# Alternating the full and the half products of a wide matrix product, and a pair of one-column products at the head of each MLP quarter

## The chip, the cores and the metric

One core of a Trainium2 chip runs the whole kernel. The metric is the device time of one execution in microseconds. PE is the matrix engine, PEld its weight loading, DVE and ACT the two engines that work on elements, POOL the general one, SP the queue that issues most loads.

## The reference

Two decoder layers over 256 tokens of 2048 features, all in float32. The first layer mixes tokens by gated linear attention, the second by windowed attention with sinks over a shared K/V. Behind each comes an MLP, which holds most of the work:

```python
def rmsnorm(x, g):
    xf = x.astype(jnp.float32)
    y = xf * lax.rsqrt(jnp.mean(xf * xf, axis=-1, keepdims=True) + EPS)
    return (y * g.astype(jnp.float32)).astype(x.dtype)

def sqrelu_mlp(h, w1, w2):
    u = jax.nn.relu(h @ w1)
    return (u * u) @ w2
...
    for layer in range(DEPTH):
        u = rmsnorm(h, norm_mix[layer])
        if layer < N_A:
            h = h + gla_mixer(u, ...)
        else:
            if layer == N_A:
                k_band, v_band = shared_kv(h, ...)
            h = h + swa_sink_mixer(u, k_band, v_band, ...)
        h = h + sqrelu_mlp(rmsnorm(h, norm_mlp[layer]), mlp_w1[layer], mlp_w2[layer])
```

`w1` is 2048 x 8192, `w2` is 8192 x 2048.

## The kernel before

Weights come from memory in blocks of 512 x 512 floats (`ws`, and `wx` and `wy` in the MLP). Each is split in two (`halve`, lines 116 and 117): ACT rounds it to the matrix engine's reduced format (`wh`), DVE takes the difference (`wl`). Activations are split in the same way (`ah`, `al`), and a full-precision product is the sum of three reduced ones, `ah*wh + ah*wl + al*wh`. All products go through the helper `mm` (line 80), so the profile shows them by their tiles: `acc<-act,wh` writes a bank of tag `acc` from activations and the high half. What stands last in such a name need not be the moving operand; the width tells.

The MLP is done in four quarters of its 8192 hidden columns. A quarter has two parts.

*Four wide products* (`gemm_wide`) make 2048 hidden columns, 512 each. A 128 x 128 block of `wh` is the stationary operand, and the two halves of the activations, `ah` and `al`, stand side by side as a moving operand of 512 columns: one full product gives `ah*wh` and `al*wh`. A second one, of 256 columns, adds `ah*wl` to one half of the bank. So each block of weights takes a pair, 512 and 256 columns. A wide product has four column blocks `f`, each with its own bank (`accs[f]`), and 16 row blocks: four steps `kq` of four `k`, hence 64 pairs. Its banks are four of tag `acc`, or two of `tp` and two of `ms` (each of those tags has a ring of two), in turn. At the end `evac_u` (line 830 on) empties each bank: ACT copies (838), DVE adds (839), relu and square follow (843, 844), and splits (847, 848).

*The seven-product part* (`seven`, called twice per quarter) multiplies the hidden columns by `w2`. Half of it is done with seven products of sums of blocks instead of eight: `product(b, o, ws)` adds operand `o` times the block `ws` to bank `b`; DVE forms sums of blocks (line 795, `wy<-wy,ws`). The other half is `plain(i, j, b0, b1)`: hidden block `i` into banks `b0` (first 128 tokens) and `b1`. `A`, `B`, `C` are `acc` banks, `D` a `tp` bank, `E` and `F` the two `ms` banks. All of its products have 512 columns. The last quarter of the second MLP has no such part; there `w2` goes through `gemm_wide` too.

The order of instructions on each engine is set when the program is built: a scheduler goes by its own estimate of when operands and banks come free, with priorities for loads and splits. `later(n, fn)` and `tick()` place small work `n` ticks ahead within the code; a wide product ticks twice in each of its four steps.

Before the change the wide products go in groups of four full products, then the four short ones of the same blocks:

Of the kernel before, what the change touches and what calls it, by code (L numbers as in the profile page):

```python
# [16 lines left out]
P = 128  # L17
# [31 lines left out]
def yoco_kernel(ctx: ExitStack, tc: tile.TileContext, x, norms, mlp_w1, mlp_w2, a_w_in, w_glr, w_gate, a_g_o, a_w_o,  # L49
# [12 lines left out]
    def bank(shape, tag, dtype=F32):  # L62
        return ps[tag].tile(shape, dtype, name=tag, tag=tag)

    def small():
        return bank([P, C], "ms")
# [4 lines left out]
    def later(n, fn):  # L71
        due.setdefault(now[0] + n, []).append(fn)

    def tick():
        now[0] += 1
        for fn in due.pop(now[0], ()):
            fn()

    def mm(o, l, r, start=True, stop=True, **kw):
        nc.tensor.matmul(o, lhsT=l, rhs=r, start=start, stop=stop, **kw)  # L80


    ident = const.tile([P, P], F32, name="ident")
# [3 lines left out]
    ones = const.tile([P, P], F32, name="ones")  # L87
# [34 lines left out]
    def split_w(parts, step=4, queue=nc.sync, between=None):  # L122
        ws = wp.tile([P, 4, C], F32, name="ws", tag="ws", bufs=WS)
        with tc.high_priority(offset=WPRI):
            for k in range(0, 4, step):
                ks = slice(k, k + step)
                o = 0
                for ap in parts:
                    n = ap.shape[1]
                    queue.dma_start(out=ws[:, ks, o:o + n],  # L130
                                    in_=ap[k * P:(k + step) * P].rearrange("(k p) n -> p k n", p=P))
                    o += n
        return halve(ws, o, min(step, 2), between)

    def piece(w, col, n=C):
        return lambda kq: [w[kq * C:(kq + 1) * C, col:col + n]]
# [55 lines left out]
    def gemm_wide(src, act, evac, last=False):  # L192


        accs = []
        tags = wide_tags[0]
        wide_tags.reverse()

        def run(kq):
            if kq == 0:  # L200
                accs.extend(bank([P, 2, T], tag) for tag in tags)
            halves = split_w(src(kq))
            ah, _, a = act[kq]

            groups = [[(k, f) for f in range(4)] for k in range(4)]
            if kq == 0:
                groups = [[(2 * k + i, 2 * h + f) for i in range(2) for f in range(2)] for h in range(2)
                          for k in range(2)]
            if last and kq == 3:
                groups = [[(k, f) for k in range(4)] for f in range(4)]  # L210
            for i, group in enumerate(groups):
                w = [[h[:, f * P:(f + 1) * P] for h in halves[k]] for k, f in group]
                for (k, f), (wh, _) in zip(group, w):
                    mm(accs[f].rearrange("p u t -> p (u t)"), wh, a[:, k].rearrange("p u t -> p (u t)"),
                       kq == 0 and k == 0, False, skip_group_check=True)
                for (k, f), (_, wl) in zip(group, w):
                    mm(accs[f][:, 1], wl, ah[:, k], False, kq == 3 and k == 3, skip_group_check=True)
                if i == 1:
                    tick()
                if last and kq == 3:  # L220
                    evac(i, accs[i])
            tick()
            if kq == 3 and not last:
                for f in range(4):
                    evac(f, accs[f])
        return run

    def go_all(run):
        for kq in range(4):
            run(kq)  # L230


    def new_act():

        a = actp.tile([P, 4, 2, T], F32R, name="act", tag="act")
        return a[:, :, 0], a[:, :, 1], a
# [54 lines left out]
    last = []  # L291
# [379 lines left out]
    def mlp(w1, w2, act, r, gains):  # L671
# [7 lines left out]
        wide_tags.sort()  # L679
        vs = [mp.tile([P, C], F32, name=f"v{n}", bufs=1) for n in range(2)]  # L680

        def new_ops():

            pairs = [actp.tile([P, 2, 2, 4, P], F32R, name="ops", tag="act") for _ in range(2)]
            return [t[:, i] for t in pairs for i in range(2)] + \
                [mp.tile([P, 2, 4, P], F32R, name=f"op{i}", bufs=1) for i in range(3)]

        def combine(op, odd, uf):

            ua, ub = (uf[c] for c in sorted(uf)[-2:]) if odd else (uf[max(uf)], None)  # L690

            def half(i, a):
                nc.scalar.copy(out=op[i][:, 0], in_=a)
                nc.vector.tensor_sub(out=op[i][:, 1], in0=a, in1=op[i].bitcast(F32)[:, 0])

            def less(a, b):
                e = mp.tile([P, 4, P], F32, name="e", tag="e")
                nc.vector.tensor_sub(out=e, in0=a, in1=b)
                return e
            if not odd:  # L700
                half(0, ua[:, :, :P])
                half(6, less(ua[:, :, :P], ua[:, :, P:]))
                return
            e = less(ua[:, :, P:], ub[:, :, P:])
            s = less(ua[:, :, :P], e)
            half(4, e)
            half(2, less(ub[:, :, :P], s))
            half(5, s)
            half(1, ub[:, :, :P])
            half(3, ub[:, :, P:])  # L710
# [110 lines left out]
        for g in range(4):  # L821
            w = w2[g * D:(g + 1) * D]
            seven_of = 0 if g == 3 and not gains else 2
            us, op, uf = {}, None, {}
            for c in range(NC4):
                if c >= seven_of:
                    us[c] = new_act()
                elif c == 0:
                    op = new_ops()
                ms = {}  # L830

                def evac_u(f, acc, c=c, ms=ms):
                    if f % 2 == 0:
                        ms[0] = mp.tile([P, 2, T], F32, name="m", tag="m")
                    if f == 0:
                        uf[c] = mp.tile([P, 4, T], F32, name="u", tag="u")
                    m, j = ms[0], f % 2
                    nc.scalar.copy(out=m[:, j], in_=acc[:, 1])
                    nc.vector.tensor_add(out=m[:, j], in0=acc[:, 0], in1=m[:, j])  # L839
                    if j == 0:  # L840
                        return
                    bs = slice(f - 1, f + 1)
                    nc.vector.scalar_tensor_tensor(out=m, in0=m, scalar=0.0, in1=rb2, op0=ALU.max, op1=ALU.mult)
                    nc.scalar.activation(out=uf[c][:, bs], in_=m, func=AF.Square)
                    if c >= seven_of:
                        ah, al, _ = us[c]
                        nc.scalar.copy(out=ah[:, bs], in_=uf[c][:, bs])
                        nc.vector.tensor_sub(out=al[:, bs], in0=uf[c][:, bs], in1=ah.bitcast(F32)[:, bs])
                    elif f == 3:
                        combine(op, c, uf)  # L850

                go_all(gemm_wide(piece(w1, g * D + c * C), act, evac_u))
            if seven_of:
                for n in range(2):
                    seven(w, n, op, us, g, g == 3 or (g == 2 and not gains), acts, gains if g == 3 else (), sq, nr)
                continue
            for c in range(NC4):
                def evac_x(f, acc, c=c):
                    d = xt[c][:, f]
                    for u in (1, 0):  # L860
                        nc.vector.tensor_add(out=d, in0=acc[:, u], in1=d)
                    r = c * C + f * P
                    nc.sync.dma_start(out=out[r:r + P], in_=d)

                if c % 2 == 0:
                    for i in range(4):
                        later(1 + i, lambda c=c + i // 2, b=i % 2: last_x(c, b, mp))
                go_all(gemm_wide(piece(w, c * C), us, evac_x, c == NC4 - 1))
# [3 lines left out]
    def last_x(c, b, mp):  # L872

        if b == 0:
            xt[c] = mp.tile([P, 4, T], F32, name="xt", tag="u")
        nc.scalar.copy(out=xt[c][:, 2 * b:2 * b + 2], in_=back(c, b))

    (actk, actq), rstd = mlp(mlp_w1[0], mlp_w2[0], actm, rm, (G_KV, G_MIX1))


# [178 lines left out]
    (actm,), rm = residual(b_w_o[0], acta, (G_MLP1,))  # L1059
    sa.close()  # L1060
    mlp(mlp_w1[1], mlp_w2[1], actm, rm, ())


# [41 lines left out]
```

## Time and profile before

| | |
|---|---|
| median of three runs | 2090.39 us (2089.78 to 2093.33) |
| the profiled execution | 2090.28 us, span 2088.6 us |
| PE busy | 2056.3 us, 98% |
| DVE, ACT busy | 1428.7 us, 1146.7 us |
| read from memory | 406.71 MB |

A row of a timeline reads: start in us, length in us, engine, line, operation, what it writes and reads, partitions x elements, count, and in brackets the idle time of the engine ahead of it and what ended that. Several like instructions are merged in a row. Products overlap in the matrix engine, so the length of one is more than its distance to the next. A row of a stretch reads: from and to, its length, PE's busy time (with the number of instructions that touch the stretch), the granted clock of PE, the mean share of the DMA engines, GB/s. A row of waits reads: who waited, for whom, us in total, times, the longest. A row of groups reads: engine, operation, operands, shapes and count, then busy us and mean ns of one, then idle time ahead of it.

### The profile page before, as it was taken

How to read it: one execution, taken by the hardware profiler on the slowest of the kernel's cores; microseconds unless marked ns; L12 is line 12 of the kernel's file. 1: busy time of each engine (PE TensorE's matmuls, PEld its weight loads, DVE VectorE, ACT ScalarE, POOL GpSimd, SP SyncE). 2: the span in 40 equal slices, each digit the busy share in tenths (PEclk: the TensorE clock that was granted, in tenths of full speed). 3: DMA queues.
4: the chain of work that ended last, by engine and by line, in shares of the span. 5: the costliest groups of instructions: out<-in, count | busy, mean ns of one | idle time of the engine just before them, and what ended most of it. 6: DMA issues, size and time to landing. Idle time of an engine off the chain costs nothing.

```text
span 2088.6 us, 26959 instructions
## 1 busy us (share of the span) xinstructions
PE 2056.3 (98%) x10734; PEld 1738.8 (83%) x10734; DVE 1428.7 (68%) x1624; ACT 1146.7 (55%) x1560; POOL 177.0 (8%) x179
## 2 busy tenths in 40 slices
PE   9999999999999999999999999999999999999999
PEld 8988888888888788888877777788788888888888
DVE  6696444567866876786797666656776786787554
ACT  6745445555655555554565676455555555555543
POOL 2262111000000000000001232000000000000000
PEclk9999999999999999999999999999999999999999
DMA  8445555656865785776675443655785686676553
GB/s 278 142 142 180 175 174 176 230 190 189 242 231 189 211 270 184 213 240 213 199 193 157 158 141 112 221 188 185 208 271 184 190 255 222 182 225 198 182 192 130
DMA packets 210654, 410.55 MB, mean 197 GB/s; under 512 B 7024, under 2 KB 15232, under 8 KB 210528
## 3 DMA queue, kind: packets, MB, share of 16 engines
q1 hardware_dynamic: 194704, 377.51, 53.8%
q0 software_dynamic: 15104, 30.23, 8.4%
q8 instruction: 84, 1.38, 0.3%
q10 hardware_dynamic: 720, 1.09, 0.2%
q14 instruction: 42, 0.34, 0.0%
HBM read 406.71 MB, written 2.10 MB: 196 GB/s over the span
## 4 chain that ended last, share of the span: by engine, by line
PE 88%; DVE 7%; ACT 3%; issue 1%; DMA 1%; POOL 0%; SPq 0%; ACTq 0%; POOLq 0%; DVEq 0%
PE acc L80 55%; PE ms L80 19%; PE tp L80 13%; DVE wl L117 3%; ACT sc L998 1%; ACT wh L116 1%; PE tp L610 1%; DVE wy L795 1%; DVE m L839 0%; PE tp L931 0%; DVE st L992 0%; DMA ws<-in_a_w_in_dram 0%; DVE st L994 0%; DMA gk<-in_b_g_q_dram 0%; PE tp L559 0%
## 5 line engine op out<-in xcount | busy, mean ns | idle before, releaser
L117 DVE TENSOR_TENSOR wl<-ws,wh 128x1024 fp32r<-128x1024 f32 (+1 forms) x636 | 780.0, 1234 | 472.5 <-ACT wh L116 467.7
L116 ACT CAST wh<-ws 128x1024 fp32r<-128x1024 f32 (+1 forms) x636 | 659.4, 1040 | 577.0 <-PE acc L80 387.6
L80 PE MATMUL acc<-wh,act 128*128 128x512 f32 x1792 | 575.5, 395 | 0.1
L80 PE MATMUL acc<-act,wh 128*128 128x512 f32 (+1 forms) x1664 | 414.1, 362 | 2.2 <-ACT wh L116 1.4
L80 PEld LDWEIGHTS acc<-wh,act 128*128 128x128 f32 x1792 | 336.2, 188 | 73.0 <-issue 3.6
L80 PE MATMUL acc<-wl,act 128*128 128x512 f32 x896 | 349.8, 391 | 0.0
L80 PEld LDWEIGHTS acc<-act,wh 128*128 128x128 f32 x1664 | 278.9, 190 | 29.7 <-ACT wh L116 1.6
L80 PE MATMUL acc<-act,wl 128*128 128x256 f32 x1408 | 257.6, 282 | 0.6 <-DVE wl L117 0.6
L80 PEld LDWEIGHTS acc<-act,wl 128*128 128x128 f32 x1408 | 227.0, 190 | 26.2 <-DVE wl L117 1.0
L80 PE MATMUL tp<-act,wh 128*128 128x512 f32 x592 | 230.1, 394 | 0.0
L80 PE MATMUL ms<-act,wh 128*128 128x512 f32 x576 | 225.9, 394 | 0.0
L80 PEld LDWEIGHTS acc<-wl,act 128*128 128x128 f32 x896 | 168.8, 188 | 35.3 <-issue 1.7
L117 DVE TENSOR_TENSOR wl<-wx,wh 128x1024 fp32r<-128x1024 f32 x112 | 135.9, 1223 | 73.1 <-ACT wh L116 71.2
L116 ACT CAST wh<-wx 128x1024 fp32r<-128x1024 f32 x112 | 117.7, 1055 | 94.3 <-PE acc L80 52.4
L80 PE MATMUL ms<-act,wl 128*128 128x256 f32 x576 | 148.6, 281 | 0.0
L80 PE MATMUL tp<-act,wl 128*128 128x256 f32 x576 | 148.3, 280 | 0.0
L80 PE MATMUL ms<-wh,act 128*128 128x512 f32 x448 | 146.0, 394 | 0.9
L730 POOL DMA_DIRECT2D wx<-in_mlp_w_dram x28 | 36.1, 1289 | 1128.4 <-DVE wl L117 1026.7
L80 PEld LDWEIGHTS tp<-act,wh 128*128 128x128 f32 x592 | 111.5, 189 | 13.3
L80 PEld LDWEIGHTS ms<-act,wh 128*128 128x128 f32 x576 | 108.6, 189 | 13.6
L80 PEld LDWEIGHTS tp<-act,wl 128*128 128x128 f32 x576 | 108.3, 189 | 12.7
L80 PEld LDWEIGHTS ms<-act,wl 128*128 128x128 f32 x576 | 108.5, 189 | 11.9
(231 smaller groups left out, 2242.9 us busy)
## 6 DMA issues: line engine op xcount, KB each, us to landing
ws<-in_mlp_w_dram SPq DMA_DIRECT2D x228, 1024.0 KB, 5.2
ws<-in_a_w_in_dram SPq DMA_DIRECT2D x44, 1024.0 KB, 5.1
wx<-in_mlp_w_dram POOLq DMA_DIRECT2D x28, 1024.0 KB, 8.9
ws<-in_a_w_o_dram SPq DMA_DIRECT2D x16, 1024.0 KB, 5.0
ws<-in_b_w_q_dram SPq DMA_DIRECT2D x16, 1024.0 KB, 5.0
ws<-in_b_w_o_dram SPq DMA_DIRECT2D x16, 1024.0 KB, 5.0
wx<-in_mlp_w_dram SPq DMA_DIRECT2D x14, 1024.0 KB, 5.1
wy<-in_mlp_w_dram SPq DMA_DIRECT2D x14, 1024.0 KB, 7.5
```

Of the source, the lines that this page charges most:

```text
L80: nc.tensor.matmul(o, lhsT=l, rhs=r, start=start, stop=stop, **kw)
L116: h = nc.scalar.copy(out=wh[:, js, :o], in_=ws[:, ks, :o])
L117: l = nc.vector.tensor_sub(out=wl[:, ks, :o], in0=ws[:, ks, :o], in1=wh.bitcast(F32)[:, js, :o])
L610: nc.tensor.transpose(out=tp[:, j, t], in_=xs[c][:, t, (2 * b + j) * P:(2 * b + j + 1) * P], identity=ident)
L730: nc.gpsimd.dma_start(out=ws, in_=block(i, j).rearrange("(k p) n -> p k n", p=P), accum_op=ALU.add)
L795: nc.vector.tensor_add(out=y, in0=y, in1=b12)
L998: nc.scalar.activation(out=sc[:, h], in_=sc[:, h], func=AF.Exp, bias=nmx[:, h:h + 1], scale=f[:, h:h + 1], accum_out=su[:, h:h + 1])
```

## The change

In `gemm_wide` the groups of four are gone: each full product is followed at once by the short one of the same block. The order of the blocks and the places of the ticks are the same. And at the first tick of each quarter of both MLPs, `pause` runs two products of one column in float32, of the identity and a column of ones, into a bank of tag `ms` that nobody reads.

```diff
-            groups = [[(k, f) for f in range(4)] for k in range(4)]
+            order = [(k, f) for k in range(4) for f in range(4)]
             if kq == 0:
-                groups = [[(2 * k + i, 2 * h + f) for i in range(2) for f in range(2)] for h in range(2)
-                          for k in range(2)]
+                order = [(k, 2 * h + f) for h in range(2) for k in range(4) for f in range(2)]
             if last and kq == 3:
-                groups = [[(k, f) for k in range(4)] for f in range(4)]
-            for i, group in enumerate(groups):
-                w = [[h[:, f * P:(f + 1) * P] for h in halves[k]] for k, f in group]
-                for (k, f), (wh, _) in zip(group, w):
-                    mm(accs[f].rearrange("p u t -> p (u t)"), wh, a[:, k].rearrange("p u t -> p (u t)"),
-                       kq == 0 and k == 0, False, skip_group_check=True)
-                for (k, f), (_, wl) in zip(group, w):
-                    mm(accs[f][:, 1], wl, ah[:, k], False, kq == 3 and k == 3, skip_group_check=True)
-                if i == 1:
+                order = [(k, f) for f in range(4) for k in range(4)]
+            for i, (k, f) in enumerate(order):
+                wh, wl = (w[:, f * P:(f + 1) * P] for w in halves[k])
+                mm(accs[f].rearrange("p u t -> p (u t)"), wh, a[:, k].rearrange("p u t -> p (u t)"),
+                   kq == 0 and k == 0, False, skip_group_check=True)
+                mm(accs[f][:, 1], wl, ah[:, k], False, kq == 3 and k == 3, skip_group_check=True)
+                if i == 7:
                     tick()
...
+        def pause():
+
+            pt = small()
+            for i in range(2):
+                mm(pt[:, i:i + 1], ident, ones[:, 0:1])
...
             us, op, uf = {}, None, {}
+            later(1, pause)
             for c in range(NC4):
```

The built order of the engines moves in two places. On PE at the start of the second quarter of the first MLP, before (the number behind a name tells tiles apart, `acc_4914` and `acc_4915` are the banks of the first two column blocks):

```order
L80 MATMUL acc_4914<-act_3169,wh_4920 128x512 [waits Activation_49]
L80 MATMUL acc_4915<-act_3169,wh_4920 128x512
L80 MATMUL acc_4914<-act_3169,wh_4920 128x512
L80 MATMUL acc_4915<-act_3169,wh_4920 128x512
L80 MATMUL acc_4914<-act_3169,wl_4922 128x256 [waits DVE_49]
L80 MATMUL acc_4915<-act_3169,wl_4922 128x256
L80 MATMUL acc_4914<-act_3169,wl_4922 128x256
L80 MATMUL acc_4915<-act_3169,wl_4922 128x256
```

and after, the end of the first eight pairs with the one-column products:

```order
L80 MATMUL acc_4917<-act_3169,wh_4924 128x512
L80 MATMUL acc_4917<-act_3169,wl_4925 128x256
L80 MATMUL acc_4918<-act_3169,wh_4924 128x512
L80 MATMUL acc_4918<-act_3169,wl_4925 128x256
L80 MATMUL ms_4946<-ones_86,ident_79 128x1 x2
L80 MATMUL acc_4919<-act_3169,wh_4923 128x512
```

Full and short products alternate, and the one-column products stand between the eighth pair and the ninth.

On PE where the first seven-product part begins, behind the product A, before (`ms_4362` is bank E, `ms_4363` bank F; `act_3953` with `wh_4355` and `wh_4356` is `plain(2, 1)`, `ops_3530` the sum matrix, `act_4141` is `plain(3, 1)`; each row stands ahead of its three to six products of the same bank and operand):

```order
L80 MATMUL ms_4362<-wh_4355,act_3953 128x512 [waits DVE_49]
...
L80 MATMUL ms_4362<-wh_4356,act_3953 128x512
...
L80 MATMUL ms_4362<-wh_4390,ops_3530 128x512 [waits Activation_49]
...
L80 MATMUL ms_4362<-wh_4414,act_4141 128x512 [waits Activation_49]
L80 MATMUL ms_4362<-wl_4416,act_4141 128x512 [waits DVE_49]
...
L80 MATMUL ms_4363<-wh_4355,act_3953 128x512 [waits DVE_49,PE_49]
```

and after (`ms_4365` is E, `ms_4366` F):

```order
L80 MATMUL ms_4365<-wh_4358,act_3956 128x512 [waits DVE_49]
...
L80 MATMUL ms_4366<-wh_4358,act_3956 128x512 [waits DVE_49]
...
L80 MATMUL ms_4365<-wh_4359,act_3956 128x512
...
L80 MATMUL ms_4365<-wh_4393,ops_3530 128x512 [waits Activation_49]
...
L80 MATMUL ms_4365<-wh_4417,act_4144 128x512 [waits Activation_49]
L80 MATMUL ms_4365<-wl_4419,act_4144 128x512 [waits DVE_49]
```

The products of `plain(2, 1)` on F, which stood behind those of the sum matrix and the first six of `plain(3, 1)`, now stand ahead of both, in turn with those on E.

On DVE at the same place, before (`m` is the emptying of the wide product's banks, `wy<-wy,ws` the sum of two matrices):

```order
L839 TENSOR_TENSOR m<-tp,m 128x256
L117 TENSOR_TENSOR wl<-wy,wh 128x1024 x2
L843 SCALAR_TENSOR_TENSOR m<-m,rb 128x512
L795 TENSOR_TENSOR wy<-wy,ws 128x2048
L848 TENSOR_TENSOR act<-u,act 128x2x256
L117 TENSOR_TENSOR wl<-ws,wh 128x1024 x2
L839 TENSOR_TENSOR m<-ms,m 128x256
```

and after:

```order
L842 TENSOR_TENSOR m<-tp,m 128x256
L846 SCALAR_TENSOR_TENSOR m<-m,rb 128x512
L117 TENSOR_TENSOR wl<-ws,wh 128x1024
L842 TENSOR_TENSOR m<-ms,m 128x256
L846 SCALAR_TENSOR_TENSOR m<-m,rb 128x512
L117 TENSOR_TENSOR wl<-wy,wh 128x1024 x2
L851 TENSOR_TENSOR act<-u,act 128x2x256
L797 TENSOR_TENSOR wy<-wy,ws 128x2048
L117 TENSOR_TENSOR wl<-ws,wh 128x1024 x2
```

The fourth bank, `m<-ms`, is emptied ahead of the sum matrix's work instead of behind all of it. The seven hand-overs are alike in this, in both orders. The other engines' rows keep their content; ACT's casts and copies move by a place or two with these, and POOL's and SP's loads stay in their order.

More of the change, by code (lines that the diff above doesn't have):

```diff
@@ L203, in run @@
             ah, _, a = act[kq]
-            groups = [[(k, f) for f in range(4)] for k in range(4)]
+            order = [(k, f) for k in range(4) for f in range(4)]
             if kq == 0:
-                groups = [[(2 * k + i, 2 * h + f) for i in range(2) for f in range(2)] for h in range(2)
-                          for k in range(2)]
+                order = [(k, 2 * h + f) for h in range(2) for k in range(4) for f in range(2)]
             if last and kq == 3:
-                groups = [[(k, f) for k in range(4)] for f in range(4)]
-            for i, group in enumerate(groups):
-                w = [[h[:, f * P:(f + 1) * P] for h in halves[k]] for k, f in group]
-                for (k, f), (wh, _) in zip(group, w):
-                    mm(accs[f].rearrange("p u t -> p (u t)"), wh, a[:, k].rearrange("p u t -> p (u t)"),
-                       kq == 0 and k == 0, False, skip_group_check=True)
-                for (k, f), (_, wl) in zip(group, w):
-                    mm(accs[f][:, 1], wl, ah[:, k], False, kq == 3 and k == 3, skip_group_check=True)
-                if i == 1:
+                order = [(k, f) for f in range(4) for k in range(4)]
[5 more added lines that the diff above has]
+                if i == 7:
                     tick()
-                if last and kq == 3:
-                    evac(i, accs[i])
+                if last and kq == 3 and k == 3:
+                    evac(f, accs[f])
             tick()
```

## The prediction

> **What bounds the kernel now.** I read the page first, then the sums over stretches of one quarter of the first MLP, then single products, then the waits.
>
> ```profile
> span 2088.6 us, 26959 instructions
> PE 2056.3 (98%) x10734; PEld 1738.8 (83%) x10734; DVE 1428.7 (68%) x1624; ACT 1146.7 (55%) x1560; POOL 177.0 (8%) x179
> PEclk9999999999999999999999999999999999999999
> PE 88%; DVE 7%; ACT 3%; issue 1%; DMA 1%; POOL 0%; SPq 0%; ACTq 0%; POOLq 0%; DVEq 0%
> ```
>
> PE has work in 98% of the span, the granted clock is at its top in every slice, and 88% of the chain that ended last is PE. So time changes in two ways only: the distance between the starts of two products changes, or a hole in PE's stream opens or closes. A busy sum does not show the first, since products overlap; distances between starts do. The next rows cut the second quarter of the first MLP into its four wide products, the first 72 products of the seven-product part, and its other 288.
>
> ```profile
> 592.44:682.25 89.81, 89.81 (x513) 1.00 0.61 198
> 682.25:700.63 18.38, 17.14 (x74) 1.00 0.77 222
> 700.63:765.91 65.28, 65.28 (x289) 1.00 0.84 246
> ```
>
> By the program the first stretch holds 256 pairs (one product of 512 columns and one of 256), so a pair takes 89.81/256 = 350.8 ns. The third holds 288 products of 512 columns at 65.28/288 = 226.7 ns, with not one hole. At that rate the 72 of the second would take 16.32 us; they take 18.38. These 2.06 us are lost seven times, at each place where wide products hand over to the seven-product part (twice four quarters, less the last, which has none): 14.4 us in all. The rows of the first such place say where:
>
> ```profile
> 516.89 0.39 PE L80 MATMUL ms<-wh,ops 128*128 128x512 f32 x1
> 517.11 0.44 PE L80 MATMUL ms<-wh,act 128*128 128x512 f32 x1
> 518.68 0.50 PE L80 MATMUL ms<-wl,act 128*128 128x512 f32 x1 [1.12 <-DVE wl L117]
> 519.01 0.63 PE L80 MATMUL ms<-wh,act 128*128 128x512 f32 x2
> 519.48 0.40 PE L80 MATMUL ms<-wl,act 128*128 128x512 f32 x1
> 519.72 0.99 PE L80 MATMUL ms<-wh,act 128*128 128x512 f32 x2
> ...
> PE ms L80 <- DVE wl L117: 9.0, 8, 1.2
> ...
> 514.60 2.29 DVE L795 TENSOR_TENSOR wy<-wy,ws 128x2048 f32<-128x2048 f32 x1
> 516.80 0.69 DVE L848 TENSOR_TENSOR act<-u,act 128x512 fp32r<-128x512 f32 x1
> 517.40 2.36 DVE L117 TENSOR_TENSOR wl<-ws,wh 128x1024 fp32r<-128x1024 f32 x2
> 519.67 0.42 DVE L839 TENSOR_TENSOR m<-ms,m 128x256 f32<-128x256 f32 x1
> ```
>
> PE needs the low part of the next matrix (of `plain(3, 1)`) at 517.3 us; DVE, which has just summed two matrices for 2.29 us, gives it from 517.40 on, and PE stands for 1.57 us between two starts (517.11 to 518.68). Three products on, it stands again, for the bank that DVE empties only at 519.67 (`m<-ms`).
>
> **The change, part by part.**
>
> *1. The hand-over.* This part is in no line of the diff, but in the order. Before, PE runs 12 products (A), 12 of `plain(2, 1)` on bank E alone, 12 of the sum matrix, and then needs `plain(3, 1)`: 36 products after the wide ones end. After, bank F is free early, so all 24 of `plain(2, 1)` run first, and `plain(3, 1)` is needed after 48. It works out as follows, from A's start (t = 0), by these rows and those above:
>
> ```profile
> 508.51 1.05 ACT L116 CAST wh<-ws 128x1024 fp32r<-128x1024 f32 x1 [1.75 <-PE ms L80]
> 510.25 0.40 ACT L838 COPY m<-ms 128x256 f32<-128x256 f32 x1
> 509.60 1.23 DVE L117 TENSOR_TENSOR wl<-ws,wh 128x1024 fp32r<-128x1024 f32 x1 [1.58 <-ACT wh L116]
> 514.00 0.69 DVE L843 SCALAR_TENSOR_TENSOR m<-m,rb 128x512 f32<-128x512 f32 x1
> ```
>
> In pair order the last full product ends about at t = 0, so ACT's cast (1.05) begins near 0.3 and the fourth bank's copy (0.40) ends near 1.75. DVE makes the low half (1.23) from 1.35 to 2.6 and empties the fourth bank (0.42) by 3.05. PE asks for that bank after 15 products, 15 x 0.227 = 3.4: 0.35 us to spare. DVE goes on: relu 0.69, two low halves of the sum matrix 2.35, `act` 0.69, the sum of matrices 2.29, the low half of `plain(3, 1)` 1.23, which is there at 10.3. PE asks for it after 48 products, at 10.9: 0.6 us to spare. ACT's own queue is off the path here (55% busy on the page). So both holes close, and the term is -7 x 2.0 = **-14 us**; a hole left by a late step costs its lateness, so its ends are -14.4 and 0. I take nearly all, since both margins come out positive. The 288 products that follow would start 2 us earlier with DMA at 0.84; they show no hole now, and I cost that at nothing (cover: the weights held ahead; if it went, the 2 us would come back there).
>
> *2. The wide products' order.* 36 wide products of 64 pairs (16 in each MLP and 4 at the end) are 2304 pairs; the records have 2320 full products of these names, 16 of them the gate's:
>
> ```profile
> L80 PE MATMUL acc<-act,wh 128*128 128x512 f32 x1152 | 316.3, 395 | 0.0
> L80 PE MATMUL tp<-act,wh 128*128 128x512 f32 x592 | 230.1, 394 | 0.0
> L80 PE MATMUL ms<-act,wh 128*128 128x512 f32 x576 | 225.9, 394 | 0.0
> ```
>
> No product is added or lost; only which follows which. A nanosecond in a pair is 2.3 us of the kernel. What a steady alternation costs stands nowhere in the trace, so I bound it by single distances:
>
> ```profile
> 592.44 1.07 PE L80 MATMUL acc<-act,wh 128*128 128x512 f32 x4
> 593.35 0.64 PE L80 MATMUL acc<-act,wl 128*128 128x256 f32 x4
> 593.82 1.09 PE L80 MATMUL acc<-act,wh 128*128 128x512 f32 x4
> ...
> 679.45 0.40 PE L80 MATMUL tp<-act,wh 128*128 128x512 f32 x1
> 679.68 0.40 PE L80 MATMUL ms<-act,wh 128*128 128x512 f32 x1
> ...
> 680.38 0.28 PE L80 MATMUL tp<-act,wl 128*128 128x256 f32 x1
> 680.49 0.28 PE L80 MATMUL ms<-act,wl 128*128 128x256 f32 x1
> ...
> 40.76 0.28 PE L80 MATMUL acc<-act,wh 128*128 128x256 f32 x1
> 40.88 0.50 PE L80 MATMUL ms<-ones,ss 128*128 128x1 f32 x4
> 41.24 0.36 PE L80 MATMUL acc<-act,wh 128*128 128x256 f32 x1
> 41.44 0.28 PE L80 MATMUL acc<-act,wl 128*128 128x256 f32 x1
> ```
>
> The first group after a run of full products takes 593.82 - 592.44 = 1.38 us, 345 ns a pair; its four full products keep the 227 ns of the run before. The groups behind it average 350.8. So PE has a better and a worse rhythm, and a run of four short products seems to throw it out of the better one. Steady runs of one kind give 227 and, in a run of short ones (40.76 to 40.88), 120 ns: 347 a pair. If one short product in between does not break the rhythm, the pair is 345 to 347: -13 to -9 us. The switches themselves, as they stand, give 0.23 us for the first full product behind a short one (679.45 to 679.68) and 0.11 to 0.12 for the first short one (680.38 to 680.49): about 350, hence -2 to 0 us. Against a gain speaks that the slow full products stand behind short ones, and in the alternation each does; the worst distances that fit these rows, 0.24 and 0.12, would be 360 and +21 us. I take 349, between the rhythm kept and the switches: 2304 x (349 - 350.8) = **-4 us**; ends -13 and +21.
>
> The nearest row on weight loading is a record of 190 ns, longer than the 120 ns from one short product to the next:
>
> ```profile
> L80 PEld LDWEIGHTS acc<-act,wl 128*128 128x128 f32 x1408 | 227.0, 190 | 26.2 <-DVE wl L117 1.0
> ```
>
> The Trainium skill (TensorE: Matmul & The Clock Gate, "LDWEIGHTS (loading the stationary operand)") puts a load at its columns over 1.2 GHz, an estimate of 107 ns for 128 columns; by that a load just hides behind a short product in either order, and this term would be 0 and the sum 4 us higher. The trace neither confirms nor refutes it, since loads and products overlap in the records.
>
> *3. The two one-column products*, eight times. The trace has four in a row: from 40.88 to 41.24, and the product behind them takes 0.20 instead of 0.12, so four cost 0.36 + 0.08 = 0.44 and two 0.22 us. Eight are **+1.8 us**; ends 1 and 4 (nothing less, since they stand in PE's own order; 4 if each pair restarted PE as dearly as four). They take one `ms` bank that nobody reads, 230 us of work ahead of any full bank, and turn the ring of two. The tick at which they run is the same as before.
>
> **The sum.** -14 - 4 + 1.8 = -16.2 against this execution's own 2090.28 us (span 2088.6 and 1.7 around it; the median of the runs is 2090.39): **2074 us**.
>
> **Rivals.**
> - *The rhythm is kept*: pairs at 345 to 347 ns. For it: the 1.38 us group; the one-column products can serve as a restart into it. Against: after that group it is lost at once. -14 - 11 + 1.8 = 2067 us.
> - *The order of wide products matters nothing or costs a little* (351 to 355 ns). For it: the switches' 350. -14 + 1 to 10 + 1.8 = 2079 to 2088 us. The rule of the Trainium skill on weight loads, above, comes out at its lower edge.
> - *The hand-over is not mended*: DVE's chain runs a microsecond longer than I add up, and the wait moves to bank F or to the low half. For it: margins of 0.35 and 0.6 us against a chain of seven steps. Without this term: 2088 us.
> - *Slower*: every full product behind a short one pays the slow start and nothing makes up for it, at 360 ns a pair: +21 - 14 + 1.8 = 2099 us. Slower than before begins where the pair exceeds 350.8 + 12.2/2.304 = 356 ns. Against: no undisturbed group in the trace averages above 352.
>
> **How the numbers follow.** Changes under 0.2% (4.2 us) cannot be told from none here. Forecast (2070 to 2079) 0.42; rhythm kept (2056 to 2070) 0.18; order neutral or dearer (2079 to 2092) 0.18; hand-over not mended (2080 to 2094) 0.14; slower (over 2094.5) 0.08. The range 2062 to 2089 leaves out the lowest third of the second case, the upper ends of the third and fourth, and the last: 2 in 10. Faster (under 2086.1): 0.42 + 0.18 + 0.13 + 0.05 = 0.78; slower 0.08 and 0.01 from the fourth; the same 0.13.
>
> **What would show it.** Right: the total of PE's waits for `wl` falls from 9.0 us to about 1 (one place of the eight is elsewhere), the first 72 products after a wide stretch take 16.3 to 16.5 us, the four wide products of a quarter take 256 x 349 = 89.3 us and 0.2 more, and the one-column rows cost 0.2 us each. Wrong: a wide stretch over 91 us, or a hole of a microsecond or more behind `ms<-wh,act`.

## The result, and the profile after

| | before | after |
|---|---|---|
| median of the runs (us) | 2090.47 (6 runs, 2089.63 to 2093.33) | 2074.9 (6 runs, 2074.45 to 2076.78) |
| the profiled execution (us) | 2090.28 | 2076.33 |
| its span (us) | 2088.6 | 2074.6 |

The ratio of the times is 0.9927, 95% interval 0.9916 to 0.9939: the change makes the kernel faster, by 15.6 us between the medians. The forecast was 2074.

First the page of the changed kernel: the span, PE's line, the granted clock and the chain of work that ended last.

```profile
span 2074.6 us, 27016 instructions
PE 2050.7 (99%) x10766; PEld 1739.6 (84%) x10766; DVE 1428.2 (69%) x1624; ACT 1152.7 (56%) x1560; POOL 175.7 (8%) x179
PEclk9999999999999999999999999999999999999999
PE 92%; DVE 4%; ACT 3%; DMA 1%; issue 1%; POOL 0%; ACTq 0%; SPq 0%; POOLq 0%; DVEq 0%
```

PE's share of the chain rose from 88% to 92%, DVE's fell from 7% to 4%: waits for DVE went. PE's busy sum fell by 5.6 us, less than the span by far, and its number of records rose by 32, which belong to the 16 one-column products (four records for each two of them, see below).

Next the second quarter of the first MLP, cut as before: its four wide products (with one time the one-column products), the first 72 products of the seven-product part, the other 288. The columns are start and end, length, PE's busy time and records, granted clock, DMA share, GB/s.

```profile
589.73:678.98 89.25, 89.25 (x518) 1.00 0.61 199
678.98:695.45 16.47, 16.47 (x75) 1.00 0.89 252
695.45:760.74 65.29, 65.29 (x290) 1.00 0.83 245
```

The 72 products take 16.47 us in place of 18.38, now without a hole. The wide stretch takes 89.25 in place of 89.81, one-column products included. The 288 behind are as they were.

The first hand-over, in DVE's and PE's rows (start, duration, instruction), and the row of PE's waits for `wl`:

```profile
509.30 1.23 DVE L117 TENSOR_TENSOR wl<-ws,wh 128x1024 fp32r<-128x1024 f32 x1
510.44 0.42 DVE L842 TENSOR_TENSOR m<-ms,m 128x256 f32<-128x256 f32 x1
...
514.38 2.29 DVE L797 TENSOR_TENSOR wy<-wy,ws 128x2048 f32<-128x2048 f32 x1
516.58 2.36 DVE L117 TENSOR_TENSOR wl<-ws,wh 128x1024 fp32r<-128x1024 f32 x2
...
508.09 0.39 PE L80 MATMUL acc<-wh,ops 128*128 128x512 f32 x1
...
518.78 0.39 PE L80 MATMUL ms<-wh,ops 128*128 128x512 f32 x1
519.01 0.39 PE L80 MATMUL ms<-wh,act 128*128 128x512 f32 x1
519.24 0.39 PE L80 MATMUL ms<-wl,act 128*128 128x512 f32 x1
...
PE ms L80 <- DVE wl L117: 1.2, 1, 1.2
```

PE starts the seven-product part at 508.09 and comes to `plain(3, 1)` at 519.01, 10.92 us later. DVE has made the first of its two low halves by about 517.8 (half of the 2.36 us behind 516.58), so PE goes on at its 227 ns. Of the 9.0 us of waits in eight places, 1.2 us in one are left.

Summed over all places in the two traces, as distances between PE's starts:

| part | before (us) | after (us) | difference |
|---|---|---|---|
| seven hand-overs: what 72 products take beyond 72 x 226.7 ns, summed | 14.42 | 0.78 | -13.64 |
| 36 wide products, one-column products included (each up to the next product's start, the last to its own end) | 814.33 | 812.52 | -1.81 |
| the rest | | | +1.5 |
| span | 2088.6 | 2074.6 | -14.0 |

The rest is what is left of the span's difference. It lies outside the MLPs, where the change touches nothing: ahead of the first MLP -0.5 us, which stays open, and between the two +1.9, which goes with the granted clock, as the last section shows. The medians of the runs differ by 15.6 us; the first two rows alone make -13.64 - 1.81 = -15.45.

### The profile page after: what moved, and what is told of

It reads as the page before. It is cut to its first block, busy times and chain, and to the rows that moved or that the text cites. A ratio compares the mean times of both kernels' runs of the same rounds, so it can differ in the third digit from the quotient of the medians.

```text
span 2074.6 us, 27016 instructions
## 1 busy us (share of the span) xinstructions
PE 2050.7 (99%) x10766; PEld 1739.6 (84%) x10766; DVE 1428.2 (69%) x1624; ACT 1152.7 (56%) x1560; POOL 175.7 (8%) x179
## 4 chain that ended last, share of the span: by engine, by line
PE 92%; DVE 4%; ACT 3%; DMA 1%; issue 1%; POOL 0%; ACTq 0%; SPq 0%; POOLq 0%; DVEq 0%
PE acc L80 56%; PE ms L80 21%; PE tp L80 13%; DVE wl L117 1%; ACT sc L1001 1%; ACT wh L116 1%; PE tp L606 1%; DMA ws<-in_a_w_in_dram 1%; PE tp L934 0%; DMA gk<-in_b_g_q_dram 0%; PE tp L555 0%; DVE po L1023 0%; DVE st L995 0%; DVE pv L1023 0%; DVE st L997 0%
## 5 line engine op out<-in xcount | busy, mean ns | idle before, releaser
L80 PE MATMUL acc<-act,wh 128*128 128x512 f32 (+1 forms) x1664 | 501.0, 362 | 2.6 <-ACT wh L116 1.9
L80 PE MATMUL acc<-act,wl 128*128 128x256 f32 x1408 | 392.3, 279 | 0.6 <-DVE wl L117 0.6
L80 PEld LDWEIGHTS acc<-act,wh 128*128 128x128 f32 x1664 | 296.7, 189 | 53.2 <-ACT wh L116 2.4
L80 PEld LDWEIGHTS acc<-act,wl 128*128 128x128 f32 x1408 | 265.9, 189 | 2.0 <-DVE wl L117 1.0
L80 PE MATMUL ms<-act,wl 128*128 128x256 f32 x576 | 161.4, 280 | 0.0
L80 PE MATMUL tp<-act,wl 128*128 128x256 f32 x576 | 159.1, 276 | 0.0
```

## The experiments

Two theories stood against each other. One: the gain is the hand-over, made by the order of the last step of the wide product before it, and the order elsewhere is worth a few microseconds. The rival: the steady rhythm of the wide products makes the gain, and the one-column products are what sets it. The first four runs take the change apart.

**Pairs without the one-column products.** The changed kernel without this line:

```diff
-            later(1, pause)
```

> The changed kernel without the one-column products. Theory (two separate terms: the hand-over's order, and a rhythm of PE in the wide products that the one-column products switch): the hand-over stays mended (72 products in 16.3 to 16.5 us), but quarters 1 to 3 of both MLPs stay in the slow rhythm of 353.3 ns a pair (a four-product stretch 90.4 us instead of 89.2); 6 x 248 pairs x 6.6 ns = +9.8, less 8 x 0.45 for the products left out = +6.2: 2081 us. Rival (alternation alone gains, the one-column products only cost): -3.6, 2071 us, pairs at 346.7.

Measured: 2074.3 us (2071.35 to 2074.63), ratio 0.9917 (0.9901 to 0.9934). This is neither expectation; it is the time of the whole change. The hand-overs cost 0.79 us in all, as with it. The second and the third quarter of the first MLP, four wide products each (columns as above):

```profile
590.10:680.53 90.43, 90.43 (x514) 1.00 0.60 196
762.28:851.09 88.81, 88.81 (x513) 1.00 0.61 200
```

256 pairs take 353.2 ns each in the one and 346.9 in the other: the same instructions in two rhythms. Most quarters fall into the fast one without any one-column product; the second of the first MLP and the first of the second MLP stay in the slow one. The place of the change can be seen. Behind the first nine pairs of most quarters PE's records show two full products in a row and then their two short ones: a swap of two neighbours that the scheduler made. First its two rows in the third quarter, then stretches of the second and the third:

```profile
765.45 0.64 PE L80 MATMUL acc<-act,wh 128*128 128x512 f32 x2
765.93 0.39 PE L80 MATMUL acc<-act,wl 128*128 128x256 f32 x2
...
593.97:680.53 86.56, 86.56 (x493) 1.00 0.58 189
762.28:765.45 3.17, 3.17 (x19) 1.00 1.03 356
766.16:851.09 84.93, 84.93 (x492) 1.00 0.59 192
```

The nine pairs ahead take 352 ns each, the 245 behind 346.7. The second quarter has the same swap, at 593.27, and its 245 pairs behind it stay at 353.3 (the first of the three stretches). All 36 wide products take 810.67 us, 1.85 less than with the one-column products. So, by the traces, these are not needed and cost more than they bring; the times of the two kernels overlap.

**One-column products alone.** The kernel before with them:

```diff
             us, op, uf = {}, None, {}
+            later(1, pause)
             for c in range(NC4):
```

> The kernel before with the one-column products added, groups of four kept. Theory: its built order has the mended hand-over too, so -13.6 + 3.6 and pairs at 350 to 351 ns: 2079 to 2081 us. Rival (the gain belongs to the alternation): the holes at the hand-over stay, 2094 us.

Measured: 2094.46 us (2092.62 to 2095.78), ratio 1.0018 (1.0008 to 1.0027). The expectation of the theory had the built order wrong: `plain(3, 1)` is still asked for after 36 products here, and the old hole is there with it. In the second quarter, the first wide product, the other three, the first 72 of the seven-product part, and PE's waits:

```profile
593.24:616.12 22.88, 22.88 (x134) 1.00 0.73 250
616.12:683.48 67.36, 67.36 (x387) 1.00 0.57 178
683.48:701.85 18.37, 17.14 (x75) 1.00 0.76 223
...
PE ms L80 <- DVE wl L117: 8.9, 8, 1.1
```

22.88 against 67.36/3 = 22.45 is the price of the two products, 0.43 us, at each of eight places; the pairs stay at 350.8 ns. They alone slow the kernel by 0.18%, some 3.8 us by the ratio.

**Pairs only in the last step before the hand-over.** The kernel before, with pairs in 16 of the 64 pairs of one wide product in each of seven quarters:

```diff
+            if tail and kq == 3:
+                groups = [[(k, f)] for k in range(4) for f in range(4)]
...
-                go_all(gemm_wide(piece(w1, g * D + c * C), act, evac_u))
+                go_all(gemm_wide(piece(w1, g * D + c * C), act, evac_u, tail=bool(seven_of) and c == 3))
```

> The kernel before, with pairs only in the last of the four steps of the last wide product of a quarter (7 x 16 of 2304 pairs), no one-column products. Theory: this alone brings the hand-over's new order and its 13.6 us: 2077 us, with the other wide products at 350.8. Rival (the gain comes from the alternation of all pairs): 2090 us.

Measured: 2077.14 us (2076.68 to 2078.04), ratio 0.9935 (0.9921 to 0.995), where the theory said 2077. The second quarter: four wide products, then the first 72 products.

```profile
590.35:680.20 89.85, 89.85 (x514) 1.00 0.60 198
680.20:696.69 16.49, 16.49 (x75) 1.00 0.86 249
```

The wide stretch is as slow as before (89.81), the hand-over is as good as after the change (16.47). 112 of 2304 pairs in the new order give 13.2 us against the kernel before in the same comparison (2090.33), of the 15.6 of the whole change.

**The reverse: the whole change, with groups of four in only that step.**

```diff
-            for i, (k, f) in enumerate(order):
...
+            size = 4 if tail and kq == 3 else 1
+            groups = [order[n:n + size] for n in range(0, 16, size)]
```

> The changed kernel with groups of four only in that last step (7 x 16 pairs); its built order has the old hand-over. Theory: pairs at 346.7 stay, the 2.06 us come back seven times: 2088 to 2089 us. Rival: 2075 us.

Measured: 2089.26 us (2087.66 to 2091.16), ratio 0.9994 (0.9985 to 1.0003). One wide product of the second quarter, its first 72 products, and the waits:

```profile
614.68:636.87 22.19, 22.19 (x131) 1.00 0.59 191
681.27:699.65 18.38, 17.15 (x75) 1.00 0.80 225
...
PE ms L80 <- DVE wl L117: 9.0, 8, 1.1
```

The fast rhythm is there (22.19) and the hole is back (18.38); the kernel's time can't be told from that before. Both directions agree: the hand-over is made by the order in that one step.

The other runs ask what the rhythm hangs on.

**Groups of two full and two short products**, without one-column products:

```diff
+            groups = [[(k, f + i) for i in range(2)] for k in range(4) for f in (0, 2)]
```

> No one-column products; wide products in groups of two full and two short ones. Theory A (rhythms: PE falls into a repeating pattern that depends on where the stream was disturbed, at best 272 and 144 cycles of 1.2 GHz, 346.7 ns a pair): a few fixed values between 346.7 and 353.4, not one for all quarters. Theory B (each full product behind a short one starts late by a fixed 7 ns): half as many switches as in pairs, so 348 to 350 everywhere. Hand-over mended in both (its last step ends like the pairs'): 2072 to 2080 us.

Measured: 2072.72 us in one run (the kernel before 2090.0 beside it). Every wide product without other work in it runs at 348.3 to 348.8 ns a pair, the 36 together take 809.21 us. One value everywhere speaks for the second theory, but its reason does not hold: groups of four have a quarter of the switches that pairs have, and take 350.8, more than any of these but the slow pairs. The cycle counts of the first theory stand in no run either; what the runs show of it is the 346.7 ns.

**One one-column product in place of two.**

```diff
-            for i in range(2):
+            for i in range(1):
```

> The changed kernel with one one-column product per quarter instead of two. Price: two cost 0.45 us in the changed kernel, so one 0.22 if the price is per product, 0.3 or more if most of it is a restart. Theory A: it may leave some quarters in the slow rhythm (353.4 ns), which ones depends on the pair it falls behind; the others at 346.7. Rival (any float32 product sets the fast rhythm): the same quarters at 346.7 as with two, 2073 us.

Measured: 2076.98 us in one run. PE's rows around the product in the second quarter:

```profile
592.69 0.28 PE L80 MATMUL acc<-act,wl 128*128 128x256 f32 x1
592.81 0.28 PE L80 MATMUL ms<-ones,ident 128*128 128x1 f32 x2
592.95 0.48 PE L80 MATMUL acc<-act,wh 128*128 128x512 f32 x1
```

One instruction leaves two records. A quarter's first wide product takes 22.47 us here and 22.69 with two, so one costs 0.22 us. It did not set the fast rhythm everywhere: the first and the last quarter of the second MLP stay at 353.3 ns. That speaks against the rival. Whether the product's place decides, as the first theory has it, is not shown: the last quarter is slow in the next run too, where nothing in it differs from pairs alone.

**A single swap of order.** Pairs without one-column products; once in one wide product (three of a quarter, in two quarters), two full products are followed by their two short ones, at no other cost:

```diff
+                todo.append((k, f, wl))
+                if swap is not None and kq == 1 and i == swap:
+                    continue
+                for k, f, wl in todo:
+                    mm(accs[f][:, 1], wl, ah[:, k], False, kq == 3 and k == 3, skip_group_check=True)
+                todo.clear()
```

> Pairs only, no one-column products; in the two quarters that stayed in the slow rhythm (second of the first MLP, first of the second MLP) two pairs at the head of the second step run as full, full, short, short, once per wide product, at the first, second and third pair (second, third and fourth wide product). Theory A: at least one of the three places switches the rhythm at no cost: from there to the end of the quarter 346.7 instead of 353.4, up to 1.2 us a quarter. Rival (only a break in the stream or a float32 product switches it): 353.4 stays.

Measured: 2072.41 us in one run. The second, third and fourth wide product of the first quarter of the second MLP:

```profile
1392.74:1415.06 22.32, 22.32 (x131) 1.00 0.57 180
1415.06:1437.55 22.49, 22.49 (x131) 1.00 0.57 189
1437.55:1459.85 22.30, 22.30 (x130) 1.00 0.51 164
```

A wide product that is slow throughout takes 22.61 and a fast one 22.19. These three change over near their first quarter, where the swap stands: to fast, back to slow, to fast. So the order of two neighbours is enough to go from one rhythm to the other, in both directions, and no break or float32 product is needed. It does not do so every time: in the other edited quarter, the second of the first MLP, the rhythm was fast ahead of the first swap and stayed so (22.20); the second and third moved it to slow and back (22.49 and 22.31).

Order alone does not set the value. The first wide product of that quarter and the last quarter of the second MLP have, in PE's records, the very same products in the same order here and in pairs alone; the one takes 22.25 us here and 22.59 there, the three wide products without other work in the other 22.61 to 22.62 here and 22.19 there.

**The best version, timed.** Groups of two again, and pairs without one-column products again, beside the kernel before on one chip.

> Wide products in groups of two full and two short ones, no one-column products, timed beside the kernel before. If the rhythm is one fixed value (348.3 ns for a pair in every wide product, as in its profile), the hand-over is worth 13.8 us, the wide products 5 us, and nothing is paid for one-column products: 2071.5 to 2073, ratio 0.991 to 0.992. If the profiled execution was a lucky one, 2074 to 2077 as with the other mended kernels.

> Wide products in single pairs, no one-column products, again, on the same chip. Quarters fall into 346.7 or 353.3 ns for a pair, and 64 pairs x 4 wide products x 6.6 ns = 1.7 us for each quarter that falls the other way: 2071 to 2076, with more spread from run to run than groups of two (which should lie within about 1 us).

Measured: groups of two 2070.91 us (2070.42 to 2074.86), ratio 0.991 (0.9897 to 0.9924); pairs 2076.09 us (2073.43 to 2079.53), ratio 0.9935 (0.9921 to 0.9948). A quarter of the first MLP and three wide products of the second, in groups of two:

```profile
590.99:680.19 89.20, 89.20 (x513) 1.00 0.61 199
1396.99:1463.87 66.88, 66.88 (x386) 1.00 0.56 178
```

Both are 348.4 ns a pair or less, in places where single pairs stay slow; the value is a fixed one, as expected. The pairs fell into the same rhythms quarter by quarter as in their first run, with 810.68 us in the wide products. So the wide products explain 1.5 us between these two kernels in the profiled executions, whose spans are 2073.2 and 2073.7. The other 3.7 us between the medians and the spread of 6 us of the pairs stay open: the rhythms of the executions without a trace are not known. In groups of two the slowest execution is the one with the lowest mean granted clock (0.995, the others 0.997 and 0.998); in pairs the clock does not sort them. Against the change itself groups of two save 3.3 us in the wide products by the traces (809.21 against 812.52); the two ratios' intervals overlap.

## Why the prediction was right, point by point

*The hand-over: -14 forecast, -13.64 measured.* The working held step by step in the rows of the first place. From PE's start at 508.09, DVE has emptied the fourth bank at 510.86, t = 2.8 (forecast 3.05); the low half of `plain(3, 1)` is there at t = 9.7 (forecast 10.3); PE comes to it at 10.92 (forecast 10.9). Both margins were larger than worked out. (One reading of the rows before was off, and no term hangs on it: PE's second stand, for the fourth bank, comes five products behind the first, not three.) The runs with pairs in the last step alone and everywhere else show that this term is separate from the rest. Its cover held as well: the 288 products behind take 65.28 us in the traces of both kernels. The rival "not mended" is what the reverse run built, and its 2089.26 us is near the 2088 worked out for it.

*The wide products' order: -4 forecast, about -5.4 measured* (the -1.81 of the table, less 3.6 for the one-column products). That is 348.5 ns a pair in the mean, where 349 was taken. In pairs alone the 36 wide products gain 814.33 - 810.67 = 3.66 us, so 1.75 of the 5.4 came with the one-column products, nearly all of it in the second quarter of the first MLP, which is fast with them and slow in pairs alone. Whether they made it so is not shown; it began fast without them in the run with a single swap. The size is right, the picture behind it is not: after the change, wide products run at two values and, behind a quarter's first pairs, at nothing between. These are wide products of the second quarter of the first MLP and of the first quarter of the second:

```profile
612.42:634.60 22.18, 22.18 (x130) 1.00 0.60 192
...
1396.27:1418.88 22.61, 22.61 (x131) 1.00 0.57 180
```

64 pairs in 22.18 and in 22.61 us are 346.6 and 353.3 ns. The rival of the kept rhythm holds in most quarters and the dearer order in a few; the mean lies where the forecast put it between them. On this row the rule of the Trainium skill that was weighed (TensorE: Matmul & The Clock Gate, "LDWEIGHTS (loading the stationary operand)") does not decide: by it either order would do, and here one and the same order ran at 346.7 and at 353.3 ns.

*The one-column products: +1.8 forecast, +3.6 measured.* This is the step that failed. It took the row `ms<-ones,ss ... x4` as four products, and so two as half of its price. The row of the changed kernel shows that two products make four records, with the same cost that was worked out for that row:

```profile
592.42 0.28 PE L80 MATMUL acc<-act,wl 128*128 128x256 f32 x1
592.54 0.50 PE L80 MATMUL ms<-ones,ident 128*128 128x1 f32 x4
592.90 0.48 PE L80 MATMUL acc<-act,wh 128*128 128x512 f32 x1
593.22 0.28 PE L80 MATMUL acc<-act,wl 128*128 128x256 f32 x1
```

0.36 us from 592.54 to 592.90, and 0.32 for the full product behind in place of 0.23: 0.45 us, eight times. The value was inside the ends of 1 and 4. The code would have told: `norm_x` calls two such products where the trace counts four. Against pairs alone the one-column products cost 1.85 us net, near the forecast, but only because the 1.75 above stands against their price.

*The sum.* -13.64 - 5.4 + 3.6 = -15.4, and -15.6 between the medians. The errors of the second and the third term, -1.4 and +1.8, nearly cancel, so that 2074 is as near as it is by luck; the first term, which carries the sum, was right in its working. No restart by the one-column products was in the sum, and the times show none: without them they are 2074.3 and 2076.09 in two comparisons, with them 2074.9.

## What to carry to other kernels

Where two stages meet, follow each buffer's release through the helpers' queues to the product that asks for it: an edit of 16 pairs in the last step before the meeting gave nearly all that the change of 2304 pairs gave. Before a row of records is used as a price, count the instructions in the code that made it. When an order of products is to be chosen for its rhythm, time several in the kernel itself and look at each stage, since a mean of 348 can be a mixture, and an order whose value is the same in every stage can be worth more than one that is faster in most (by the traces 809.21 us for groups of two here, 810.67 for pairs).

## What the runs showed of the hardware that was not expected

Products of 512 and 256 columns, each with a weight load of its own, have several steady rhythms at a granted clock of 1.00, by order and by what went before: 346.7 or 353.3 ns a pair in alternating pairs, 348.3 in groups of two, 350.8 (in one place 350.0) in groups of four. A single swap of two neighbours moved the alternating pairs from one of their values to the other at five of six places. The same order ran at either value in different kernels. What in PE sets the value was not found.

Between the MLPs lie 1.9 us that the change did not make, and the granted clock accounts for them. At two places there PE stands idle in all of the traces: about 4.5 us for `rv`, and some 30 us later 2 us for `khl`. Behind such a place the products can run at half the clock for a while. Two stretches of after, one for each place, then PE's row at the second:

```profile
1119.15:1125.97 6.82, 5.03 (x14) 0.50 0.16 34
1149.87:1153.28 3.41, 3.41 (x16) 0.50 0.95 304
...
1149.85 0.75 PE L934 MATMUL tp<-identr,khl 128*128 128x128 f32 x4 [1.97 <-ACT khl L948]
```

And the same of before:

```profile
1131.54:1134.95 3.41, 3.41 (x11) 0.50 0.09 8
1159.15:1162.56 3.41, 3.41 (x24) 1.00 0.95 302
...
1159.15 0.54 PE L931 MATMUL tp<-identr,khl 128*128 128x128 f32 x4 [1.98 <-ACT khl L945]
```

Behind `rv` the clock is 0.50 for 6.82 us after and for 3.41 before. Six of the eleven traces have the long fall and five the short one, and from the end of the 72 products of the fourth hand-over to `khl` PE takes 112.3 to 112.8 us in the six, 111.4 to 111.7 in the five. Behind `khl` the clock is 0.50 for 3.41 us after and stays at 1.00 before; the hundred products from there on take 21.54 us in place of 20.22.

The traces also show when the clock falls at `khl`. Within each trace the changes of the clock lie on a grid of 3.41 us (in that of after, the falls at 1149.87 and 1303.47 are 9 and 54 such steps behind the one at 1119.15). PE's idle time there is 1.97 to 1.98 us in all eleven traces. In six of them, after among them, 1.96 us of it or more falls into one step of the grid, and the clock is 0.50 in the next. In the other five a boundary divides it, with at most 1.80 us in either step (1.67 and 0.31 in before), and the clock stays at 1.00. So the same idle time costs 1.3 us or nothing by where it falls on the grid, and two executions of one kernel can differ by that: pairs alone had no fall there in its first trace (20.20 us for the hundred products) and one in its second (21.59).
